# Hybrid attention and DeltaNet step on one core: values of head pair 1 ahead of the keys of pair 2, and no clearing of the diagonal blocks

## The chip, the core and the metric

The kernel runs on one core of a Trainium2 chip. It is one launch; its time is the device time of that launch in microseconds, as the median of some runs. TensorE (PE), VectorE (DVE), ScalarE (ACT), GpSimd (POOL) and SyncE (SP, which here only issues DMAs) each work off their own queue in order and wait for one another by semaphores.

## What is computed

A two-layer decoder trunk for a prompt of 1024 tokens and a sample group of 8 sequences with 4 tokens each, all of width 1024. Layer 0 is sliding-window attention, layer 1 gated DeltaNet with 8 query/key heads and 16 value heads of 128; each branch has a SiLU gate. The change touches layer 1 for the prompt, cut here to what matters:

```python
xqkv, z, a, b = split(h @ w_in)
q, k, v = split(silu(short_causal_conv(xqkv)))
q, k = l2_norm(q), l2_norm(k)                      # 8 heads, each used by two value heads
lower = where(strict, (k_i . k_j) beta_i exp(gc_i - gc_j), 0)
w = triangular_solve(lower + I, [v beta, k beta exp(gc)])
u = w_v - w_k @ S                                  # chunk by chunk
o = (q exp(gc)) @ S + (q k^T decay) @ u
S = S exp(g_total) + k_decayed^T @ u
y = (rms_norm(o) * silu(z)) @ w_out
```

The reference uses chunks of 64 tokens; the kernel does the same sum with 8 chunks of 128 (`NB`).

## The kernel before

The kernel computes in fp32. Its large products split both operands into a high and a low part of type fp32r and add three matmuls (`h2hi` with `wh`, `h2lo` with `wh`, `h2hi` with `wl`). The input of layer 1 lies in SBUF, transposed, in three token groups of 384, 384 and 288 columns (`GRP`). A projection of 128 output columns is therefore 8 x 3 matmuls for each group, 72 in all. Its weights come as two loads of 256 KB (`wr`); ACT rounds them to `wh`, POOL makes `wl`.

Layer 1 goes by head pairs: pair r is one query/key head and two value heads. For each pair the kernel needs these stages:

- `proj_kq` projects a key (k) or a query (q), `proj_v` the two values (here v1a and v1b for pair 1), `proj_z` one gate (z2 and z3 for pair 1). `conv` (L1655) takes a projection from PSUM on ACT (`XR`), applies the four taps (`taps`, one on ACT and three on DVE, into `kT`, `qT` or `vT`) and a SiLU; for the samples (`samples`) it takes a small path over PE, POOL and some small DMAs. The `vT` tiles are transposed into `vo` (`turn`).
- `decay_blocks` makes the decay matrices `DP`. `solve` (L1832) computes the norms of the keys and the 8 triangular systems `UZ` (two heads by 128 x 128, four tiles of four systems) as `UZ<-ps_lg,sj,DP`. It writes the 32 x 32 blocks on the diagonals of all systems to DRAM (`Ld`).
- `invert` (L1882) loads them as `X` (64 small systems side by side), sets their diagonals to one on POOL, and inverts them by 31 pairs of DVE instructions (`tmp<-X`, `X<-X,tmp`), which follow one another through a single buffer. The result goes through DRAM (`Xdd`) into `Xc`. Before the change POOL also clears the diagonal blocks of `UZ` here (L1892 to L1896): 16 memsets for each pair.
- `diagonal` (L1914) and `blocks` (L1936), together the block solve: POOL spreads `Xc` into `Xd`, a tile that is zero outside its diagonal blocks; PE multiplies `UZ` by it (`ps_lg<-Xd,UZ`); ACT negates the product into `M`; DVE transposes `Xd` over the whole of `UZ`. Then six rounds of small products (`ps_lg<-UZ,M`), which DVE copies back into `UZ`, fill the blocks off the diagonal.
- `decayed` makes the query-key matrices in `DP`.
- `chain` (L1984) goes through the 8 chunks of a pair in order: PE multiplies key by state (`ps_mi<-S,kT`), DVE corrects the values (`vo<-ps_mi,nEg,vo`), PE applies the solved system (`ps_ob<-vo,UZ`), DVE scales the result (`us<-ps_ob,sd`), PE multiplies it by the keys (`ps_mi<-us,ktok`), DVE makes the next state (`S`). `output` adds `ps_mi<-S,qT` and `ps_mi<-uo,DP`; `gating` normalises the output on ACT, DVE and POOL (`rst`, `fo`), transposes it (`ps_tr<-cst,vo`) and gates it.

The order of all this is made while the program is built. `Core` (L96) keeps a clock for each engine with rough costs, and every helper is a generator that says when it could go on. Projections are the main line: after each matmul the waiting generators may put their instructions into the queues. Two words matter. `weave` adds a generator to those that wait. `until(condition)` holds the main line: as long as the condition is false, only generators add instructions, so nothing of the main line stands among them in PE's queue.

The main line of layer 1 is the loop over r at L2157. Round r starts with the chain of pair r - 1 and the query of pair r, then two gates, then the key of pair r + 1 and the two values of pair r, in the order that `VK` picks:

```python
for what in "vk" if r in VK else "kv":
    if what == "k":
        until(lambda: finished[0] >= r - 1)
        proj_kq(r + 1, states[r + 1], (0,))
    else:
        until(lambda: gs is not None and gated[0] >= 4 * (r - 1))
        proj_v(r, states[r])
```

So the key of pair r + 1 is held until the chain of pair r - 1 is finished (its tiles are used again), and the values of pair r until pair r - 2 is gated. `plan` (L1633) puts the weight loads into the same order. The chain of a pair needs its values and the first tile of its solved systems; the block solve of a pair needs its keys.

Of the kernel before, what the change touches and what calls it, by code (L numbers as in the profile page):

```python
# [219 lines left out]
def body(tc, I, O, cst_ap, dbg=None):  # L220
    nc = tc.nc
# [22 lines left out]
    SW = (1, 16)  # L244
    MS = (32, 15)
    AH, AI = (a / 10 for a in AM)
    VK = ()
    MM = (0, 20)
    ORDER = [("q", 2), ("q", 3), ("q", 4), ("q", 5), ("z", 0), ("k", 1), ("z", 1), ("z", 2), ("q", 6), ("q", 7),
             ("z", 3), ("z", 4), ("z", 5), ("z", 6), ("z", 7)]  # L250
# [234 lines left out]
    def weave(gen, name, hq=None):  # L485

        rank = KR[hq][name] if hq is not None else K[name]
        i = 0
        while i < len(jobs) and jobs[i][3] <= rank:
            i += 1  # L490
        jobs.insert(i, [lambda: True, gen, name, rank])
# [25 lines left out]
    def plain():  # L517
        return not isinstance(nc, Core)

    def ready(*ts):  # L520
        return lambda: plain() or nc.ready(ts) <= nc.free["tensor"]

    def soon(*ts):
        return lambda: plain() or nc.ready(ts) <= nc.free["tensor"] + AH

    def idle(eng, *ts):
        return lambda: plain() or max(nc.free[eng], nc.ready(ts)) <= nc.free["tensor"] + AI
# [7 lines left out]
    def bank(tag):  # L535

        q = held.setdefault(tag, [])
        yield lambda: len(q) < banks[tag] or q[-banks[tag]] is None
        t = psb(tag)
        q.append(t.tensor.name)  # L540
        yield lambda: plain() or nc.after(nc.used, t, "tensor") <= nc.free["tensor"]
        return t

    def give(tag, t):
        q = held[tag]
        q[q.index(t.tensor.name)] = None
# [215 lines left out]
    if True:  # L762
# [524 lines left out]
        nc = Core(tc)  # L1287
# [346 lines left out]
    for r in range(HQ):  # L1634
        pz, pv = [4096 + 2 * r * P, 4096 + (2 * r + 1) * P], [2 * HQ * P + 2 * r * P, 2 * HQ * P + (2 * r + 1) * P]
        pk = [(HQ + r + 1) * P]
        plan += [r * P] + (pz + (pv + pk if r in VK else pk + pv) if r + 1 < HQ else pv + pz)
    hhi, hlo = h2hi, h2lo
# [4 lines left out]
    if True:  # L1643
# [163 lines left out]
        def spare(hq):  # L1807

            return "mi" if hq == 0 else "lg"
# [22 lines left out]
        def solve(hq, st):  # L1832
# [25 lines left out]
            for c4 in range(2):  # L1858
# [19 lines left out]
                give(lg, pk)  # L1878
            st["built"] = True
            weave(invert(hq, st, Ld, Xdd), "invert", hq)  # L1880

        def invert(hq, st, Ld, Xdd):  # L1882
            UZ, lg = st["UZ"], spare(hq)
            yield lambda: inverted[0] == hq


            X = gs.tile([64, 32, 32], F32, tag="X", name="X")
            tmp = gs.tile([64, 256], F32, tag="tmp", name="tmp")
            nc.sync.dma_start(X, Ld)
            yield soon(X)  # L1890
            nc.gpsimd.memset(X.rearrange("p i c -> p (i c)")[:, 0:1024:33], 1.0)
            for cp_ in range(4):  # L1892
                uv = UZ[cp_].rearrange("p h c i -> p (h c) i")
                for b in range(4):
                    bs = slice(32 * b, 32 * b + 32)
                    nc.gpsimd.memset(uv[bs, :, bs], 0.0)  # L1896
            yield soon(X)
            for k in range(31):
                n, m = 31 - k, k + 1
                tv = tmp[:, 0:n * m].rearrange("p (i c) -> p i c", c=m)  # L1900
                yield idle("vector")
                nc.vector.tensor_tensor(tv, X[:, k, k + 1:].unsqueeze(2).to_broadcast([64, n, m]),
                                        X[:, k, 0:m].unsqueeze(1).to_broadcast([64, n, m]), ALU.mult)
                nc.vector.tensor_tensor(X[:, k + 1:, 0:m], X[:, k + 1:, 0:m], tv, ALU.subtract)
            nc.sync.dma_start(Xdd, X)
            inverted[0] += 1
            yield lambda: solved[0] == hq
            Xc = gs.tile([P, 16, 32], F32, tag="Xc", name="Xc")
            for b in range(4):
                nc.sync.dma_start(Xc[32 * b:32 * b + 32], Xdd[16 * b:16 * b + 16].rearrange("q i c -> i q c"))  # L1910

            lg, Ms, uzs = "lg", [], [t_.rearrange("p h c i -> p (h c) i") for t_ in UZ]

            def diagonal():  # L1914

                for cp_, uz in enumerate(uzs):
                    xd = Xd[cp_ % 2]
                    yield soon(Xc)
                    for b in range(4):
                        bs = slice(32 * b, 32 * b + 32)  # L1920
                        nc.gpsimd.tensor_tensor(xd[bs, :, bs], Xc[bs, 4 * cp_:4 * cp_ + 4, :],
                                                C["lo32"][bs, :].unsqueeze(1).to_broadcast([32, 4, 32]), ALU.mult)
                    yield lambda: st.get("pairs", 0) >= cp_ - 2
                    yield ready(xd)
                    pm = yield from bank(lg)
                    pmv = pm.rearrange("p (q i) -> p q i", q=4)
                    for q in range(4):
                        nc.tensor.matmul(pmv[:, q, 0:96], uz[:, q, :], xd[:, q, 0:96], start=True, stop=True)
                    yield soon(pm)
                    M = gs.tile([P, 4, 96], F32, tag="M", name="M", bufs=3)  # L1930
                    nc.scalar.activation(M, pmv[:, :, 0:96], AF.Copy, scale=-1.0)
                    give(lg, pm)
                    nc.vector.transpose(uz.rearrange("p q i -> p (q i)"), xd.rearrange("p q i -> p (q i)"))
                    Ms.append(M)

            def blocks():  # L1936


                for v in range(6):
                    parts = [(v - s, 64 - 32 * s) for s in range(3) if 0 <= v - s < 4]  # L1940
                    yield lambda: len(Ms) > parts[0][0]
                    yield ready(*[Ms[cp_] for cp_, _ in parts], *[UZ[cp_] for cp_, _ in parts])
                    pz = yield from bank(lg)
                    pzv = pz.rearrange("p (q i) -> p q i", q=4)
                    for q in range(4):
                        for cp_, r0 in reversed(parts):
                            rs, cs = slice(r0, r0 + 32), slice(r0 + 32, P)
                            nc.tensor.matmul(pzv[rs, q, cs], Ms[cp_][:, q, rs], uzs[cp_][:, q, cs], start=True, stop=True,
                                             skip_group_check=True)
                    yield soon(pz)  # L1950
                    for cp_, r0 in reversed(parts):
                        rs, cs = slice(r0, r0 + 32), slice(r0 + 32, P)
                        nc.vector.tensor_copy(uzs[cp_][rs, :, cs], pzv[rs, :, cs])
                    give(lg, pz)
                    st["pairs"] = max(0, v - 1)
                solved[0] += 1

            weave(blocks(), "blocks", hq)
            weave(diagonal(), "blocks", hq)

        def decayed(hq, st):
# [195 lines left out]
        for r in range(HQ):  # L2157
# [5 lines left out]
            if r + 1 < HQ:  # L2163
# [4 lines left out]
                weave(solve(r + 1, states[r + 1]), "solve", r + 1)  # L2168
                for what in "vk" if r in VK else "kv":
                    if what == "k":  # L2170
# [509 lines left out]
    nc = nc.nc  # L2680
# [36 lines left out]
```

## Time and profile before

| | |
|---|---|
| runs before | 1739.1, 1732.38, 1730.36 us; median 1732.38 |
| the profiled execution, its own time | 1730.22 us |
| its span | 1728.1 us |
| mean granted PE clock | 0.983 |

A profile's times count from the start of its span. In rows of instructions the columns are start, length, engine, line, operation, output and inputs by the program's names, shapes and count, then the idle time of the engine before them and what ended it. Nearly all instructions have line 89, the wrapper that records them, so rows are told apart by their tiles. An fp32 product appears as two records; a row with x4 can be two of them. Rows of groups give the count, busy time in us and the mean of one in ns.

### The profile page before, as it was taken

Reading aid. Unit: us, or ns where it says so; the run is one execution under the profiler, and the core shown is the slowest. Engines: PE = TensorE matmul, PEld = TensorE weight load, DVE = VectorE, ACT = ScalarE, POOL = GpSimd, SP = SyncE. Lnnn points to the kernel's source line nnn. Section 1 sums busy time; section 2 is a strip of 40 time slices with the busy share of each in tenths; the row PEclk is TensorE's granted clock in tenths of the full one; section 3 lists DMA queues with packets and bytes.
Section 4 is the critical chain, followed back from the end, with each engine's and each line's share of the span. In section 5 each row is a group of like instructions: output and inputs, shape, how many; then the busy total and the mean of one; then the engine's idle time right before and its main releaser. Section 6 shows DMA issues by size and latency. Waiting matters only on the chain. (4 is left out here: it accounts for less than half of the span.)

```text
span 1728.1 us, 31800 instructions
## 1 busy us (share of the span) xinstructions
PE 1628.6 (94%) x10666; PEld 1432.1 (83%) x10666; DVE 1207.9 (70%) x3538; ACT 862.0 (50%) x2514; POOL 603.2 (35%) x1170
## 2 busy tenths in 40 slices
PE   6999999998999899799999999999999998989897
PEld 5988888986777889689989999899998996667685
DVE  4526675564565678877887789778798876357677
ACT  4625555444334565256554665654756555332332
POOL 2601111112122334354443544545345454332322
PEclk9999999999999999899999999999999999999999
DMA  9542121233233232132412323224232137764785
GB/s 330 152 134 72 52 58 50 55 98 106 85 130 103 81 79 67 53 88 56 126 36 75 102 59 107 69 77 112 50 107 62 46 97 211 228 200 130 233 277 184
DMA packets 281573, 191.77 MB, mean 111 GB/s; under 512 B 98362, under 2 KB 253882, under 8 KB 281379
## 3 DMA queue, kind: packets, MB, share of 16 engines
q1 hardware_dynamic: 281410, 189.75, 38.1%
q8 instruction: 84, 1.38, 0.3%
q14 instruction: 79, 0.64, 0.1%
HBM read 144.68 MB, written 47.04 MB: 111 GB/s over the span
## 5 line engine op out<-in xcount | busy, mean ns | idle before, releaser
L89 PE MATMUL ps_pj<-h2hi,wl 128*128 128x384 f32 (+1 forms) x1128 | 380.4, 337 | 2.2 <-POOL wl L89 2.2
L89 PE MATMUL ps_pj<-h2hi,wh 128*128 128x384 f32 (+1 forms) x1128 | 378.3, 335 | 2.1 <-ACT wh L89 2.1
L89 PE MATMUL ps_pj<-h2lo,wh 128*128 128x384 f32 (+1 forms) x1128 | 379.4, 336 | 0.0
L89 POOL TENSOR_TENSOR wl<-wr,wh 128x512 fp32r<-128x512 f32 x122 | 164.4, 1348 | 517.5 <-ACT wh L89 432.9
L89 PEld LDWEIGHTS ps_pj<-h2hi,wl 128*128 128x128 f32 x1128 | 213.6, 189 | 6.2 <-POOL wl L89 3.1
L89 PEld LDWEIGHTS ps_pj<-h2hi,wh 128*128 128x128 f32 x1128 | 213.5, 189 | 4.3 <-ACT wh L89 2.4
L89 PEld LDWEIGHTS ps_pj<-h2lo,wh 128*128 128x128 f32 x1128 | 213.5, 189 | 3.2
L89 POOL TENSOR_TENSOR xt<-xt,y 128x512 f32<-128x512 f32 (+1 forms) x48 | 63.9, 1333 | 188.2 <-DVE y L89 165.1
L89 PE MATMUL ps_pj<-hlo,wh 128*128 128x384 f32 (+1 forms) x360 | 119.0, 331 | 0.0
L89 PE MATMUL ps_pj<-hhi,wh 128*128 128x384 f32 (+1 forms) x360 | 118.4, 329 | 0.0
L89 PE MATMUL ps_pj<-hhi,wl 128*128 128x384 f32 (+1 forms) x360 | 117.9, 328 | 0.0
L89 DVE SCALAR_TENSOR_TENSOR vT<-XR,cT,vT 128x384 f32<-128x384 f32 (+1 forms) x144 | 93.0, 658 | 29.0 <-ACT vT L89 27.1
L89 DVE TENSOR_TENSOR tmp<-X 64x31 f32<-64x31 f32 (+15 forms) x248 | 94.0, 379 | 10.4 <-POOL X L89 7.1
L89 DVE TENSOR_TENSOR X<-X,tmp 64x31 f32<-64x31 f32 (+15 forms) x248 | 94.6, 381 | 8.5
L89 ACT CAST wh<-wr 128x512 fp32r<-128x512 f32 x122 | 75.1, 616 | 16.4 <-PE ps_pj L89 12.0
L89 PEld LDWEIGHTS ps_pj<-hlo,wh 128*128 128x128 f32 x360 | 67.7, 188 | 11.2 <-issue 11.1
L89 ACT COPY XR<-ps_pj 128x384 f32<-128x384 f32 (+1 forms) x96 | 43.0, 448 | 55.9 <-PE ps_pj L89 55.7
L89 POOL TENSOR_TENSOR Xd<-Xc,cst 32x128 f32<-32x128 f32 x128 | 63.4, 495 | 21.2 <-DMA Xc<-Xdd 10.4
L89 PEld LDWEIGHTS ps_pj<-hhi,wh 128*128 128x128 f32 x360 | 67.7, 188 | 2.7 <-issue 2.7
L89 ACT ACTIVATE prob<-prob,nm 128x256 f32<-128x256 f32 (+1 forms) x128 | 62.2, 489 | 14.8 <-DVE nm L89 14.6
L89 PEld LDWEIGHTS ps_pj<-hhi,wl 128*128 128x128 f32 x360 | 67.7, 188 | 2.1 <-issue 2.1
L89 ACT ACTIVATE vo<-vo,fo 128x128 f32<-128x128 f32 x128 | 42.3, 392 | 54.0 <-POOL fo L89 54.0
(574 smaller groups left out, 4218.1 us busy)
## 6 DMA issues: line engine op xcount, KB each, us to landing
wr<-in_gdn_w_in SPq DMA_DIRECT2D x96, 256.0 KB
S<-in_state_gdn_s SPq DMA_DIRECT2D x40, 256.0 KB
xt<-in_x_prompt SPq DMA_DIRECT2D x16, 512.0 KB
wm<-in_w_mod SPq DMA_DIRECT2D x16, 512.0 KB
wr<-in_swa_w_in SPq DMA_DIRECT2D x64, 128.0 KB
wmod<-in_w_mod SPq DMA_DIRECT2D x32, 256.0 KB
wm<-in_w_mod SPq DMA_DIRECT2D x32, 256.0 KB
DP<-gcr SPq DMA_DIRECT2D x64, 128.0 KB
```

The source lines that it names most:

```text
L89: inst = fn(*args, **kwargs)
```

## The change

`VK` names the rounds in which the values go first. It was empty and now holds 1: in round 1 the order q1, z2, z3, k2, v1a, v1b becomes q1, z2, z3, v1a, v1b, k2, for the weight loads too. And `invert` no longer clears the diagonal blocks of `UZ`, for any pair. Where the zeros were read, their product gets other numbers in the rows of its own block; these are later multiplied by blocks of `UZ` that are still zero, so the result is the same. The blank line that the diff adds in `diagonal` has no meaning.

```diff
@@ -244,7 +244,7 @@
     SW = (1, 16)
     MS = (32, 15)
     AH, AI = (a / 10 for a in AM)
-    VK = ()
+    VK = (1,)
     MM = (0, 20)
@@ -1889,11 +1889,6 @@
             nc.sync.dma_start(X, Ld)
             yield soon(X)
             nc.gpsimd.memset(X.rearrange("p i c -> p (i c)")[:, 0:1024:33], 1.0)
-            for cp_ in range(4):
-                uv = UZ[cp_].rearrange("p h c i -> p (h c) i")
-                for b in range(4):
-                    bs = slice(32 * b, 32 * b + 32)
-                    nc.gpsimd.memset(uv[bs, :, bs], 0.0)
             yield soon(X)
             for k in range(31):
                 n, m = 31 - k, k + 1
```

As the order follows from the clocks of `Core`, every queue differs behind these places: the built orders of the two kernels agree up to the first 3165 of PE's 7724 entries.

## The prediction

> **What bounds the kernel now.** I read the page first, then the windows by round, then the timelines of TensorE (PE), VectorE (DVE) and GpSimd (POOL) where a round is longer than the others.
>
> ```profile
> span 1728.1 us, 31800 instructions
> PE 1628.6 (94%) x10666; PEld 1432.1 (83%) x10666; DVE 1207.9 (70%) x3538; ACT 862.0 (50%) x2514; POOL 603.2 (35%) x1170
> ```
>
> PE is busy in 94% of the span, far ahead of the rest, so what counts is where PE's queue stands still. Matmul spans overlap, so idle time alone understates it; rounds show it better. A round is what the kernel issues from one query projection to the next: six projections of 72 matmuls and the other pairs' work between them. Its borders (658.0, 797.4, 908.6, ...) are where the matmuls that write `ps_pj` go from 288 columns back to 384 for a query group. The columns of the windows view are window, length, busy time of PE, weight loads, DVE, ACT, POOL, then clock, DMA share, GB/s.
>
> ```profile
> 658.00:797.40 139.40, 125.42 (x896) 112.80 (x896) 114.74 (x313) 67.06 (x207) 57.43 (x142) 0.96 0.26 69
> 797.40:908.60 111.20, 107.45 (x755) 101.65 (x754) 90.33 (x251) 62.13 (x195) 50.12 (x126) 0.98 0.30 78
> 908.60:1019.10 110.50, 107.86 (x759) 102.83 (x758) 87.50 (x247) 62.40 (x197) 49.45 (x126) 0.98 0.32 83
> 1019.10:1128.70 109.60, 107.35 (x761) 100.73 (x760) 92.62 (x251) 65.07 (x203) 51.95 (x126) 1.00 0.30 80
> 1128.70:1235.70 107.00, 105.62 (x751) 99.41 (x750) 84.45 (x234) 62.30 (x198) 50.55 (x126) 1.00 0.30 83
> 1235.70:1346.80 111.10, 107.57 (x764) 101.31 (x763) 94.64 (x261) 61.26 (x194) 50.41 (x126) 1.00 0.31 81
> ...
> 705.20:754.10 48.90, 38.21 (x280) 29.30 (x281) 40.00 (x122) 17.09 (x62) 14.74 (x52) 0.90 0.19 51
> 754.10:797.40 43.30, 42.95 (x311) 41.01 (x310) 33.89 (x82) 30.21 (x87) 16.53 (x34) 1.00 0.25 67
> ```
>
> Round 1, the one that the change reorders, takes 139.4 us; the next five take 109.9 on average ((111.2 + 110.5 + 109.6 + 107.0 + 111.1) / 5). The surplus of 29.5 us sits in 705.2 to 754.1: clock 0.90, and no projection matmul in 48.9 us. There the kernel waits, while it is built, until the chain of pair 0 is finished before it may write the keys of pair 2 into PE's queue, so PE has only that chain, step by step behind DVE, and the rest of two block solves.
>
> ```profile
> 720.48 0.75 PE L89 MATMUL ps_ob<-vo,UZ 128*128 128x128 f32 x4 [0.58 <-DVE vo L89]
> ...
> 726.91 0.75 PE L89 MATMUL ps_ob<-vo,UZ 128*128 128x128 f32 x4 [0.44 <-DVE vo L89]
> ...
> 733.13 0.75 PE L89 MATMUL ps_ob<-vo,UZ 128*128 128x128 f32 x4 [0.44 <-DVE vo L89]
> ...
> 737.40 0.74 PE L89 MATMUL ps_ob<-vo,UZ 128*128 128x128 f32 x4 [0.44 <-DVE vo L89]
> 738.85 0.70 PE L89 MATMUL ps_mi<-us,ktok 128*128 128x256 f32 x2 [0.70 <-DVE us L89]
> ...
> 740.51 0.60 PE L89 MATMUL ps_mi<-S,qT 128*128 128x256 f32 x2
> 740.95 0.61 PE L89 MATMUL ps_mi<-uo,DP 128*128 128x128 f32 x4
> 741.39 1.03 PE L89 MATMUL ps_lg<-Xd,UZ 128*128 128x96 f32 x8
> 742.26 0.62 PE L89 MATMUL ps_mi<-S,kT 128*128 128x256 f32 x2
> ...
> 743.68 0.44 PE L89 MATMUL ps_lg<-UZ,M 128*32 128x32 f32 x8
> ...
> 745.15 0.61 PE L89 MATMUL ps_lg<-UZ,M 128*32 128x64 f32 x16 [0.39 <-DVE UZ L89]
> ...
> 748.53 0.85 PE L89 MATMUL ps_lg<-UZ,M 128*32 128x96 f32 x24
> ...
> 754.11 0.42 PE L89 MATMUL ps_pj<-h2hi,wh 128*128 128x384 f32 x1
> ```
>
> One step of the chain runs from one `ps_ob<-vo,UZ` to the next: 733.13 to 737.40 is 4.3 us when DVE is free, 720.48 to 726.91 is 6.4 us while DVE also works at the inversion of pair 1. At 754.11 the keys of pair 2 begin.
>
> **The change part by part.** Part one: the two value projections of pair 1 go ahead of the keys of pair 2. They need no finished chain, so in the built order the chain of pair 0 now lies between the matmuls of z3, v1a and v1b.
>
> ```profile
> 697.39 0.29 PE L89 MATMUL ps_pj<-h2hi,wh 128*128 128x288 f32 x1
> 697.52 0.30 PE L89 MATMUL ps_pj<-h2lo,wh 128*128 128x288 f32 x1
> ...
> 754.72 0.34 PE L89 MATMUL ps_pj<-h2hi,wh 128*128 128x384 f32 x1
> 754.89 0.34 PE L89 MATMUL ps_pj<-h2lo,wh 128*128 128x384 f32 x1
> ```
>
> A projection is 48 matmuls of 384 columns, 0.17 to 0.18 us apart, and 24 of 288, 0.13 apart: 48 x 0.175 + 24 x 0.13 = 11.5 us. The two bring 23 us of cover. What can be won is what round 1 loses: the 29.5 us less the work that it has beyond a usual round. That is one more block solve, since pairs 0 and 1 are both solved there: four groups of `Xd,UZ` at 0.87 (741.39 to 742.26) and six of `UZ,M`, two each of 0.44, 0.61 and 0.85 (743.68, 745.15, 748.53), 3.5 + 3.8 = 7.3. So 22.2 us can go, and 23 us of cover is just enough: term -22.2.
>
> First cost: the end of the chain still stands bare. In the built order the last two steps of pair 0 come after the last matmul of v1b with nothing between them: 24 operations, each two records in the trace. On an unloaded DVE they take a step (4.3) and the piece from 737.40 to the end of `uo,DP` at 740.95 + 0.61, 4.2: 8.5 us. Their own work is 5 products 256 wide at 0.44 (740.51 to 740.95) and 19 operations 128 wide at 0.22 (two in 740.95 to 741.39), 6.4. Lost: 2.1; with step and tail both slowed as 6.4 to 4.3, 12.7, it is 6.3. I take 3.5, as the inversion of pair 1 ends about there. Queued behind it on PE are the keys of pair 2, and behind those the system of pair 2.
>
> Second cost: what is late next. The keys of pair 2 come two projections later, but chain 1 does not move with them. In the built order the block solve of pair 2 slips from k3 and v2a into q3 and z6, and the chain of pair 2 starts in z6 instead of q3. The keys of pair 4 wait for that chain, so behind z7 stands a second bare stretch: 34 operations, two and a half steps. By the same rows it lasts 2 x 4.3 + 2.7 = 11.3 (2.7 from `us,ktok` at 738.85 to 741.56) to 2 x 6.4 + 2.7 = 15.5, and holds 8 x 0.44 + 26 x 0.22 = 9.2 of work. Lost: 2.1 to 6.3; I take 4.5, because half of the inversion of pair 3 stands among those steps.
>
> Third cost: DVE. Its taps of the two value convolutions now lie among the steps of chain 0.
>
> ```profile
> L89 DVE SCALAR_TENSOR_TENSOR vT<-XR,cT,vT 128x384 f32<-128x384 f32 (+1 forms) x144 | 93.0, 658 | 29.0 <-ACT vT L89 27.1
> ...
> L89 DVE COPY UZ<-ps_lg 32x128 f32<-32x128 f32 (+2 forms) x96 | 40.0, 417 | 9.9 <-PE ps_lg L89 7.9
> ...
> L89 DVE STREAM_TRANSPOSE UZ<-Xd 128x512 f32<-128x512 f32 x32 | 22.7, 709 | 18.4 <-PE ps_lg L89 15.7 <-POOL fo L89 1.2 <-POOL Xd L89 1.1
> ```
>
> Two projections have 18 of the 144 taps: 18 x 0.658 = 11.8 us. The copies and transposes of one block solve move out to q2: 12 x 0.417 + 4 x 0.709 = 7.8. Between the first and the last scaling of chain 0
>
> ```profile
> 709.34 0.61 DVE L89 TENSOR_SCALAR us<-ps_ob,sd 128x128 f32<-128x128 f32 x2
> ...
> 750.78 0.61 DVE L89 TENSOR_SCALAR us<-ps_ob,sd 128x128 f32<-128x128 f32 x2
> ```
>
> lie 41.4 us; DVE needs 4.0 more, about 45. PE's queue holds, by the built order, 96 projection matmuls of 384 columns and 55 of 288 between the same points (24.0), 20 wide products (8.8), 56 operations 128 wide (12.3) and the end of a block solve (0.9): 46. Two engines equally full, with a chain that goes to and fro between them, lose something: 0, or half of the added taps, 6. I take 3.
>
> Part two: GpSimd's clears.
>
> ```profile
> 691.93 3.71 POOL L89 MEMSET UZ<- 32x128 f32 x16
> 695.71 4.35 POOL L89 TENSOR_TENSOR Xd<-Xc,cst 32x128 f32<-32x128 f32 x8
> ```
>
> Sixteen clears hold POOL from 691.93 to 695.71, 3.8 us for each pair, and the next `Xd` of the block solve of pair 0 stands right behind them. Without them that solve can come up to 3.8 us sooner. Elsewhere PE waits little for POOL:
>
> ```profile
> PE ps_lg L89 <- POOL Xd L89: 4.2, 3, 1.9
> ...
> PE ps_pj L89 <- POOL wl L89: 2.2, 2, 1.5
> ```
>
> The cover is now z3's and v1a's matmuls, so I take 0, bounds 0 and -3.8; without cover the whole 3.8 counts once. Nothing else needs the zeros: the product that read them is later multiplied by rows that are zero. DVE doesn't gain either: the same multiplication of the inversion takes 0.29 at 694.73, with the clears beside it, and 0.29 at 728.04, with none.
>
> ```profile
> 694.73 0.29 DVE L89 TENSOR_TENSOR tmp<-X 64x135 f32<-64x135 f32 x1
> ...
> 728.04 0.29 DVE L89 TENSOR_TENSOR tmp<-X 64x135 f32<-64x135 f32 x1
> ```
>
> The moved projections take their transfers along: each has two weight loads of 256 KB, one load of old convolution state and five small stores on SP, and its two `wl` splits and eight sample operations on POOL. Weights are planned in the same changed order, and from 705.2 to 754.1 the DMA engines are 0.19 and POOL 14.74 of 48.9 us busy, so they cost nothing; if that cover failed, one late split costs what the longest wait for `wl` is, 1.5 us.
>
> Sum: -22.2 + 3.5 + 4.5 + 3 + 0 = -11.2. The profiled execution took 1730.2 us, its span of 1728.1 and 2.1 around it, so 1719.0. The three runs lie at 1730.4, 1732.4 and 1739.1, the profile at their lower end, where a run of the changed kernel can come out as well: 1719.
>
> [...] In 705.2 to 754.1 the clock is 0.90 and four records of `uo,DP` take 0.61 at 740.95. [...]
>
> **The rivals.** Full cover, 1708: both bare ends cost their lower bound, the block solve comes forward and DVE hides its taps: -22.2 + 2.1 + 2.1 - 3.8 = -21.8. For it: PE's rounds 2 to 6 run close to their work. Against: the two bare ends stand in the built order.
>
> The wait only moves, 1728: DVE, not missing PE work, holds chain 0. Then the 11.8 us of taps lengthen that chain in full, the bare ends cost what I take for them, and -22.2 + 11.8 + 3.5 + 4.5 = -2.4. For it: DVE is busy 40.0 of the 48.9 us. Against: the step from 733.13 takes 4.3 where the one from 720.48 takes 6.4, so the chain alone leaves DVE room.
>
> Slower, 1742: pair 2 becomes the late one. Its inversion stands behind chain 1 on DVE.
>
> ```profile
> L89 DVE TENSOR_TENSOR tmp<-X 64x31 f32<-64x31 f32 (+15 forms) x248 | 94.0, 379 | 10.4 <-POOL X L89 7.1
> L89 DVE TENSOR_TENSOR X<-X,tmp 64x31 f32<-64x31 f32 (+15 forms) x248 | 94.6, 381 | 8.5
> ```
>
> Per pair that is (94.0 + 94.6) / 8 = 23.6 us of DVE, followed by a block solve and eight steps of 6.4, all before the keys of pair 4. If the chain of pair 2 ends some 30 us after z7's last matmul, the old loss of 22.2 is back in round 3, with the first bare end (6.3) and the dense DVE (6) on top: -22.2 + 22.2 + 12.3 = +12.3, and from there on it decides. Against: only two and a half steps stand bare behind z7, not eight.
>
> **How the numbers follow.** Forecast 0.50, full cover 0.12, wait moves 0.22, slower 0.16. The likeliest case's own range follows from its bounds: -22.2 + 2.1 + 2.1 + 0 - 3.8 to -22.2 + 6.3 + 6.3 + 6 is 1708 to 1727. 0.5%, what a measurement of this kernel can tell from no change, is 8.7 us: below 1723.7 is faster, above 1741 slower. Faster: most of the forecast (0.44), full cover (0.12) and a little of the third, 0.58. Slower: 0.15. Within: 0.27. The 8-in-10 range goes from just under full cover to near the slower case, 1707 to 1740.
>
> **What would show it.** Right: round 1 near 118 us instead of 139.4, with z3, v1a and v1b matmuls between the steps of chain 0 and a clock near 1.00; a bare stretch under 10 us before the keys of pair 2 and one of 11 to 15 us before the keys of pair 4; rounds 4 to 6 as before; no POOL clears of `UZ`. Wrong: a bare stretch of 25 us or more in round 3 (slower), steps of 8 us in round 1 with PE waiting for `us` and `vo` (wait moves), or a gain spread over all rounds, which would mean that the clears were on the path.

## The result and the profile after

The changed kernel takes 1722.28 us in the median of 5 runs (1719.15 to 1723.84), the kernel before 1736.34 of 5 (1730.36 to 1739.1). The ratio is 0.9921 with a 95% interval of 0.9897 to 0.9946: 13.7 us, with 9.4 to 17.9 as bounds. A second comparison, `changed_again` below, gives 0.9931 (0.9912 to 0.9949). The profiled execution took 1723.84 us.

The head of the changed kernel's page, span and busy times:

```profile
span 1721.9 us, 31655 instructions
PE 1630.3 (95%) x10666; PEld 1435.0 (83%) x10666; DVE 1210.1 (70%) x3538; ACT 862.9 (50%) x2514; POOL 587.1 (34%) x1042
```

PE, DVE and ACT have as many instructions as before. POOL has 128 fewer, the clears, which kept it busy for 25.2 us before; its busy time falls by only 16 us, as its other instructions together took 9 us longer. The windows of the changed kernel by round, cut as before at the first matmul of each query (columns as in the prediction), and below them its two bare stretches:

```profile
664.40:783.70 119.30, 112.62 (x831) 104.95 (x830) 102.14 (x269) 58.93 (x184) 55.84 (x126) 1.00 0.30 79
783.70:889.60 105.90, 102.16 (x682) 97.78 (x681) 86.96 (x248) 67.88 (x215) 45.90 (x98) 0.98 0.31 84
889.60:1015.80 126.20, 120.27 (x899) 110.14 (x899) 105.77 (x287) 63.83 (x198) 53.31 (x122) 0.99 0.27 72
1015.80:1124.00 108.20, 107.78 (x761) 101.04 (x760) 91.78 (x252) 64.95 (x202) 48.26 (x110) 1.00 0.31 82
1124.00:1230.80 106.80, 106.15 (x758) 100.71 (x758) 88.62 (x246) 63.19 (x199) 48.83 (x110) 1.00 0.32 82
1230.80:1337.60 106.80, 106.06 (x756) 100.42 (x755) 87.73 (x251) 61.69 (x194) 47.31 (x110) 1.00 0.30 83
1337.60:1412.50 74.90, 73.28 (x470) 68.80 (x469) 66.82 (x181) 48.69 (x164) 36.77 (x90) 1.00 0.24 67
753.30:763.50 10.20, 6.63 (x40) 4.78 (x38) 6.02 (x22) 6.86 (x28) 5.38 (x20) 1.00 0.64 161
949.60:963.50 13.90, 11.04 (x59) 8.74 (x58) 9.27 (x33) 6.72 (x30) 4.63 (x17) 0.88 0.43 102
```

Round 1 falls from 139.4 to 119.3 us with a clock of 1.00 in place of 0.96, round 2 from 111.2 to 105.9, and round 3 grows from 110.5 to 126.2. The chain of pair 0 now runs between projection matmuls, as PE's timeline of the changed kernel shows:

```profile
726.03 0.60 PE L89 MATMUL ps_ob<-vo,UZ 128*128 128x128 f32 x4
726.39 0.42 PE L89 MATMUL ps_pj<-h2hi,wh 128*128 128x384 f32 x1
...
732.52 0.61 PE L89 MATMUL ps_ob<-vo,UZ 128*128 128x128 f32 x4
...
753.24 0.29 PE L89 MATMUL ps_pj<-h2hi,wl 128*128 128x288 f32 x1
...
753.77 0.61 PE L89 MATMUL ps_ob<-vo,UZ 128*128 128x128 f32 x4
755.91 0.70 PE L89 MATMUL ps_mi<-us,ktok 128*128 128x256 f32 x2 [1.52 <-DVE us L89]
...
759.03 0.75 PE L89 MATMUL ps_ob<-vo,UZ 128*128 128x128 f32 x4 [0.45 <-DVE vo L89]
...
763.06 0.60 PE L89 MATMUL ps_tr<-cst,vo 128*128 128x128 f32 x4
763.42 0.42 PE L89 MATMUL ps_pj<-h2hi,wh 128*128 128x384 f32 x1
```

A step of the chain takes 6.5 us there (726.03 to 732.52), and PE works on projections meanwhile. The last matmul of v1b starts at 753.24, the keys of pair 2 at 763.42: between them stand the last two steps, bare, for 10.2 us.

**One number for the lost time.** A round also changes when work moves in or out of it. So the experiments use a second measure as well: for every matmul of a round, the time until the next one starts, less the median of that time over all matmuls of its kind (same product, same width) in that trace, where that is positive; the sum is the *loss* of the round. Before, round 1 lost 33.1 us and rounds 2 to 6 lost 13.7 on average (15.2, 14.6, 13.2, 11.4, 14.2). After, round 1 lost 19.1, rounds 2 and 3 together 36.2 (29.8 before), rounds 4 to 7 together 42.2 (47.2 before): 110.1 in rounds 1 to 7 became 97.5. The loss of a shorter stretch is summed in the same way.

Rounds and losses of all kernels, one profile each, in us. The ratios are of all runs, each profile is of one: that of `clears_charged_not_run` is the longest of its 12 runs, that of `values_first_1_3_and_5` the shortest of its 12. "Last" is the time from the first matmul of z15 to the end of the span:

| kernel | ratio to before (95%) | r1 | r2 | r3 | r4 to r7 | r1 to r7 | last | loss r1 | loss r2 + r3 | loss r4 to r7 |
|---|---|---|---|---|---|---|---|---|---|---|
| before | 1 | 139.4 | 111.2 | 110.5 | 402.1 | 763.2 | 306.9 | 33.1 | 29.8 | 47.2 |
| changed | 0.9921 (0.9897, 0.9946) | 119.3 | 105.9 | 126.2 | 396.7 | 748.1 | 309.4 | 19.1 | 36.2 | 42.2 |
| changed_again | 0.9931 (0.9912, 0.9949) | 119.5 | 106.0 | 125.7 | 396.1 | 747.3 | 307.7 | 19.3 | 35.7 | 41.6 |
| order_only | 1.0049 (1.003, 1.0068) | 121.1 | 118.7 | 113.8 | 409.2 | 762.8 | 315.8 | 20.9 | 37.3 | 54.8 |
| no_clears_only | 1.0107 (1.0082, 1.0131) | 141.1 | 114.2 | 109.3 | 415.5 | 780.1 | 307.2 | 35.3 | 31.8 | 59.0 |
| clears_charged_not_run | 0.9979 (0.9965, 0.9993) | 138.6 | 111.0 | 110.9 | 400.1 | 760.6 | 309.3 | 32.1 | 29.9 | 45.1 |
| changed_with_clears_uncharged | 0.998 (0.996, 1.0001) | 123.7 | 108.9 | 125.5 | 401.3 | 759.4 | 305.5 | 23.2 | 38.2 | 46.5 |
| order_only_clears_charged_not_run | 0.9993 (0.9975, 1.0011) | 122.3 | 119.6 | 112.2 | 399.5 | 753.6 | 314.7 | 22.3 | 36.6 | 44.9 |
| values_first_1_and_3 | 0.9985 (0.9971, 0.9999) | 119.4 | 103.8 | 117.3 | 409.2 | 749.7 | 315.5 | 19.1 | 29.5 | 52.6 |
| values_first_1_3_and_5 | 1.0001 (0.9985, 1.0018) | 121.2 | 104.0 | 117.6 | 419.2 | 762.0 | 302.2 | 20.8 | 29.7 | 60.7 |
| changed_without_taps_of_pair_1 | 0.9914 (0.9889, 0.9939) | 118.5 | 106.6 | 125.2 | 397.0 | 747.3 | 308.7 | 18.3 | 35.9 | 42.5 |
| one_value_first | 1.0168 (1.0151, 1.0186) | 130.2 | 113.3 | 125.5 | 413.3 | 782.3 | 308.1 | 26.9 | 41.9 | 56.9 |
| outputs_of_pair_1_later | 0.9941 (0.9922, 0.9961) | 119.1 | 113.9 | 116.3 | 398.2 | 747.5 | 307.3 | 18.9 | 34.9 | 42.7 |
| chain_of_pair_1_later | 1.0083 (1.0063, 1.0104) | 119.2 | 110.7 | 118.7 | 420.7 | 769.3 | 312.2 | 19.0 | 33.8 | 63.9 |

### The profile page after: what moved, and what is told of

The parts are those of the page before. It is cut to its first block, busy times and chain, and to the rows that moved or that the text cites. A ratio compares the mean times of both kernels' runs of the same rounds, so it can differ in the third digit from the quotient of the medians.

```text
span 1721.9 us, 31655 instructions
## 1 busy us (share of the span) xinstructions
PE 1630.3 (95%) x10666; PEld 1435.0 (83%) x10666; DVE 1210.1 (70%) x3538; ACT 862.9 (50%) x2514; POOL 587.1 (34%) x1042
## 5 line engine op out<-in xcount | busy, mean ns | idle before, releaser
L89 PE MATMUL ps_pj<-hlo,wh 128*128 128x384 f32 (+1 forms) x360 | 119.3, 331 | 0.0
L89 DVE SCALAR_TENSOR_TENSOR vT<-XR,cT,vT 128x384 f32<-128x384 f32 (+1 forms) x144 | 96.8, 680 | 25.1 <-ACT vT L89 23.8
L89 DVE TENSOR_TENSOR tmp<-X 64x31 f32<-64x31 f32 (+15 forms) x248 | 97.7, 394 | 7.2 <-POOL X L89 3.9
L89 PEld LDWEIGHTS ps_pj<-hlo,wh 128*128 128x128 f32 x360 | 67.9, 189 | 11.2 <-issue 11.1
L89 ACT ACTIVATE prob<-prob,nm 128x256 f32<-128x256 f32 (+1 forms) x128 | 62.2, 489 | 14.8 <-DVE nm L89 14.6
L89 ACT ACTIVATE qe<-ps_mi,Eg 128x128 f32<-128x128 f32 x112 | 35.0, 364 | 66.4 <-PE ps_mi L89 66.4
```

The lines of the kernel that those rows point to most:

```text
L89: inst = fn(*args, **kwargs)
```

## The experiments

Each of the two parts also changes what the kernel's own clocks charge, and so the order of everything behind it. The first runs separate three things: the order, the clears on the chip, and the charge for the clears.

**The first part alone.** `VK` is changed, the clears stay.

```diff
-    VK = ()
+    VK = (1,)
```

> Only the first half of the change: the values of pair 1 go ahead of the keys of pair 2, GpSimd keeps its clears. In the built order 24 operations stand bare behind v1b as in the changed kernel, but no stretch of 34 behind z7. Theory (the gain is the filled wait of round 1, the clears are worth nothing): -22.2 + 3.5 + 3 = about -15.7 us against the kernel before, ratio 0.991, round 1 near 119 us and round 3 near 118 instead of the 126.2 of the changed kernel. Rival one (the clears are the gain): ratio 1.000, with round 1 shortened and the time lost again in rounds 2 and 3. Rival two (the stretch behind z7 costs nothing): ratio as the changed kernel, 0.992, and round 3 no shorter than its 126.

Measured: 1743.59 us against 1735.03, ratio 1.0049. Round 1 came near to what was expected, 121.1 us. Round 3, without the stretch behind z7, took 113.8 where 118 was expected, but round 2 took 118.7, rounds 4 to 7 took 7.1 us more than before, and the last stage 8.9 more. The theory holds for round 1; the sum made of it falls. By its number the first rival is the nearest. A run below, with this order and without the clears, shows that about 9.7 us of this kernel's time are the clears; what else it lost behind round 1 came with the new order.

**The second part alone.** The five lines of the clears go, `VK` stays empty.

> Only the second half of the change: the clears go, the keys stay ahead of the values. The charge of the clears on the kernel's own clocks goes too, so the order is made anew: behind z3 now stand 79 operations without a projection matmul instead of 146. Theory (what counts is how long the chain of pair 0 stands without projections): the loss of 22.2 us shrinks with the number of operations, 22.2 x 79 / 146 = 12.0, so about -10 us, ratio 0.994, all of it in round 1. Rival one (the clears themselves hold the solves): 3.8 us in each of eight pairs, up to -30 us, ratio down to 0.983, spread over the rounds. Rival two (the length of that stretch doesn't matter): 1.000.

Measured: 1752.34 us against 1735.03, ratio 1.0107. No expectation had a slower kernel; for round 1 the second rival, that the length of the stretch doesn't matter, comes out. The window of round 1 of this kernel:

```profile
662.50:803.60 141.10, 126.63 (x897) 113.34 (x897) 113.68 (x302) 66.96 (x205) 54.55 (x126) 0.95 0.27 67
```

With 79 operations bare behind z3 instead of 146 it is no shorter than before (139.4). The bare stretch itself, from the last matmul of z3 to the keys of pair 2, lasts 44.9 us (710.77 to 755.63) instead of 51.1 (702.99 to 754.11), and loses 25.6 instead of 23.9. The operations that moved out of the stretch had not made it long; they had filled it. It lasts until the chain has finished, and half the operations did not make it lose less. Another 10 us went in round 7 (84.4 against 74.4), in a new order of its own.

**The clears alone, with the order held.** The clears are charged and not issued. In the built order TensorE, VectorE, ScalarE and SyncE have the same entries in the same sequence as before.

```diff
-                    nc.gpsimd.memset(uv[bs, :, bs], 0.0)
+                    nc.issued("gpsimd", "memset", None, (uv[bs, :, bs],), {})
```

> The kernel before, but the 128 clears aren't issued, while their cost stays on the kernel's own clocks: TensorE, VectorE, ScalarE and SyncE keep the order of the kernel before, entry by entry. This is the worth of the clears on the chip alone. Theory: 0, at most -3.8 us (round 1, ahead of the block solve of pair 0): ratio 0.998 to 1.000. Rival (the clears hold every block solve): 8 x 3.8 = -30 us, ratio 0.983, or some part of that spread over the rounds.

Measured: 0.9979, 3.6 us (1.2 to 6.1). By its number the theory's lower end holds, but not by its place: round 1, where all of it was to be, gained 0.8 us. The product behind the clears of round 1 has no wait in the kernel before:

```profile
698.59 1.03 PE L89 MATMUL ps_lg<-Xd,UZ 128*128 128x96 f32 x8
```

The rest of the 3.6 us stands in no single place of the trace.

**The order of the changed kernel, with the clears.** The clears are issued and not charged, so that TensorE, VectorE and ScalarE keep the order of the changed kernel.

```diff
+            for cp_ in range(4):
+                uv = UZ[cp_].rearrange("p h c i -> p (h c) i")
+                for b in range(4):
+                    bs = slice(32 * b, 32 * b + 32)
+                    nc.quiet(nc.nc.gpsimd.memset(uv[bs, :, bs], 0.0).ins)
```

(`quiet` only keeps them in program order on GpSimd.)

> The changed kernel with the 128 clears issued again on GpSimd, but not charged on the kernel's own clocks: TensorE, VectorE and ScalarE keep the order of the changed kernel, entry by entry. It separates what the clears cost on the chip from what their charge does to the order. Theory (as with the kernel before, where the clears were worth 0.21%, 3.6 us): 0 to 6 us above the changed kernel, ratio to the kernel before 0.992 to 0.996. Rival (the clears are most of the gain of the changed kernel): back at 1.000 or above.

Measured: 0.998, between the theory and its rival. So the clears are worth 0.5 to 0.6% here, 8.5 or 10.2 us (0.998 less 0.9931 or 0.9921, of 1733), more than the 3.6 in the old order and above what the theory allowed. The intervals of the two figures meet; that the clears cost more in this order rests on the next run and on the traces as well. Rounds 1 to 7 took 759.4 instead of 748.1, and the trace shows where. POOL's timeline of this kernel, around the block solve of pair 0, then the gating in round 2:

```profile
698.01 0.16 POOL L89 MEMSET X<- 64x32 f32 x1 [1.00 <-DMA smd<-th]
698.07 3.73 POOL L1902 MEMSET UZ<- 32x128 f32 x16
701.86 4.07 POOL L89 TENSOR_TENSOR Xd<-Xc,cst 32x128 f32<-32x128 f32 x8
...
843.73 0.16 POOL L89 MEMSET X<- 64x32 f32 x1 [1.78 <-DMA X<-Ld]
843.79 3.80 POOL L1902 MEMSET UZ<- 32x128 f32 x16
847.67 0.20 POOL L89 TENSOR_TENSOR rst<-rsw 128x4 f32<-128x4 f32 x1
...
851.47 0.20 POOL L89 TENSOR_TENSOR fo<-rst,rsw 128x4 f32<-128x4 f32 x1
```

PE's timeline of the same kernel at both places:

```profile
703.38 2.03 PE L89 MATMUL ps_lg<-Xd,UZ 128*128 128x96 f32 x8 [2.41 <-POOL Xd L89]
...
852.16 1.35 PE L89 MATMUL ps_tr<-cst,vo 128*128 128x128 f32 x4 [3.53 <-ACT vo L89]
```

And the changed kernel's POOL and PE at the same two places:

```profile
697.39 0.15 POOL L89 MEMSET X<- 64x32 f32 x1 [0.99 <-DMA X<-Ld]
697.62 2.04 POOL L89 TENSOR_TENSOR Xd<-Xc,cst 32x128 f32<-32x128 f32 x4
...
837.75 0.17 POOL L89 MEMSET X<- 64x32 f32 x1 [0.90 <-DMA X<-Ld]
837.91 0.20 POOL L89 TENSOR_TENSOR rst<-rsw 128x4 f32<-128x4 f32 x1
...
841.18 0.27 POOL L89 TENSOR_TENSOR fo<-rst,rsw 128x4 f32<-128x4 f32 x1
```

```profile
700.77 1.03 PE L89 MATMUL ps_lg<-Xd,UZ 128*128 128x96 f32 x8
...
843.25 0.60 PE L89 MATMUL ps_tr<-cst,vo 128*128 128x128 f32 x4
```

With the clears the next `Xd` starts at 701.86, behind 3.73 us of memsets, and PE stands 2.41 us with the product at the head of its queue. All the matmuls of z3 that come behind it in the queue wait as well (the next one starts at 705.12): they are not cover. Without the clears the product has no wait. The place costs more than the 2.41 us of the wait: from 702.60 to 709.50 the granted clock is 0.51. The windows of the kernel with the clears:

```profile
699.20:702.60 3.40, 1.77 (x15) 1.17 (x14) 2.33 (x8) 0.15 (x1) 2.87 (x14) 1.00 0.33 108
702.60:709.50 6.90, 6.12 (x34) 5.51 (x35) 2.50 (x6) 0.49 (x1) 4.72 (x11) 0.51 0.00 0
```

In the changed kernel the clock is 1.00 there, and the same matmuls take 4.8 us less. In round 2 the sixteen clears of pair 2 stand between the diagonal of `X` and the `rst` of a gating; the gating's `fo` is late, ACT scales late, and PE waits 3.53 us for `vo`. Without them the transposition runs between the matmuls of z5 with no wait.

PE's order is the same in the two kernels but for 10 of 10666 records, so each matmul can be set against its twin. The kernel with the clears falls back by 4.8 us at the block solve and by 5.7 at the gating, of which 3.0 come back later in round 2 (the changed kernel has the clock at 0.51 from 872.7 to 876.2, the other has 1.00 at these matmuls). It falls back by 2.1 more in round 5 and by 2.9 in round 7. There the clears stand ahead of the small convolution of the samples on POOL; ACT waits for its result (`us`) with the copy of `uo` behind it in its queue, and PE waits for `uo`:

```profile
1137.60 3.83 POOL L1902 MEMSET UZ<- 32x128 f32 x16
1141.49 0.43 POOL L89 COPY XS<-XR 128x32 f32<-128x32 f32 x1
...
1144.75 0.23 ACT L89 ACTIVATE us<-us 128x32 f32<-128x32 f32 x1 [6.76 <-POOL us L89]
...
1146.71 0.71 PE L89 MATMUL ps_mi<-uo,DP 128*128 128x128 f32 x4 [1.87 <-ACT uo L89]
```

**The first order without the clears.** As `clears_charged_not_run`, with `VK = (1,)`.

> The values of pair 1 first, in the very order that the kernel with the charged clears had (ratio 1.0049), but without the clears. Theory (that kernel is slow because of its order in the later stages, not because of the clears): 1.001 to 1.005. Rival (the values-first order makes the clears harmful, so that both parts need one another on the chip): 0.992, as the changed kernel.

Measured: 0.9993 against 1.0049 for the same order with clears: 0.56%, 9.7 us. It lies between the theory and the rival. Again the clears cost about 10 us in a values-first order, though at other places: here round 1 gains nothing without them, and the loss of rounds 4 to 7 falls from 54.8 to 44.9. What the theory says of the order holds in part: without its clears this kernel is still some 11 us slower than the changed one, of which 5.3 us are in the last stage (314.7 against 309.4) and 5.5 in rounds 1 to 7.

**The taps.** For pair 1's values the three VectorE taps are charged and not issued.

```diff
-                        nc.vector.scalar_tensor_tensor(up, XR[:, a0 + i:e + i], cw[:, i, ct:ct + 1], up, ALU.mult, ALU.add)
+                        args_ = (up, XR[:, a0 + i:e + i], cw[:, i, ct:ct + 1], up, ALU.mult, ALU.add)
+                        if ct in (18, 19):
+                            nc.issued("vector", "scalar_tensor_tensor", None, args_, {})
+                        else:
+                            nc.vector.scalar_tensor_tensor(*args_)
```

> The changed kernel without the last three of the four taps of the convolution of pair 1's values (18 VectorE instructions, 11.8 us), which stay charged on the kernel's own clocks, so that all orders stay. It measures the third cost of the prediction, the taps among the steps of chain 0. Prediction: 3 us, bounds 0 and 6: ratio to the kernel before 0.989 to 0.992, round 1 at 113 to 119 instead of 119.3. Rival (VectorE holds chain 0, the wait only moves): 11.8 us, ratio 0.985 to 0.986, round 1 near 108.

Measured: 0.9914, which the intervals can't tell from the changed kernel. The window of round 1 of this kernel:

```profile
664.50:783.00 118.50, 112.53 (x829) 104.87 (x829) 93.72 (x251) 58.75 (x184) 52.83 (x126) 1.00 0.30 79
```

DVE has 18 instructions and 8.4 us less (102.14 to 93.72), and the round is 0.8 us shorter. The chain does wait for VectorE at single steps, but the added taps don't lengthen it; the rival is refuted.

**Values first in more rounds.** `VK = (1, 3)` and `VK = (1, 3, 5)`, no clears.

> The changed kernel, with the values first in round 3 too (pair 3 ahead of the keys of pair 4). In the built order the stretch of 34 operations behind z7 is gone, the 24 behind v1b stay, and no stretch of over 18 stands in the rounds after. Theory (the stretch behind z7 is the second cost, 4.5 us predicted, up to 7.8 by the trace of the changed kernel): 4.5 to 8 us below the changed kernel, ratio to the kernel before 0.988 to 0.990, round 3 near 119 us instead of 126.2. Rival one (that stretch is hidden anyway): 0.992, as the changed kernel. Rival two (the wait only moves on by two rounds each time): a stretch in round 5 costs the same again, 0.992, and round 5 is longer than 107.

> No clears, values first in rounds 1, 3 and 5. Up to the middle of round 5 its built order is that of the kernel with rounds 1 and 3, and the last stage has the order of the changed kernel. Theory (the last stage costs 298 us in the order of the changed kernel and 304 in that of rounds 1 and 3, whatever stands before): rounds 1 to 4 as with rounds 1 and 3 (119, 104, 117, 115), last stage 298, together 0.994 to 0.996. Rival one (the last stage is slower by what happened earlier, not by its own order): 304 again, 0.998. Rival two (each further swap pays as the first): below 0.992.

Measured: 0.9985 and 1.0001. Without the stretch behind z7 the loss of rounds 2 and 3 is 29.5, as before the change (29.8; 36.2 in the changed kernel). But rounds 4 to 7 lose 52.6 instead of 42.2, and the last stage takes 315.5. With round 5 swapped too, the last stage is short again, 302.2, and shorter than the theory had it (the theory's 298 and 304 count from another place; by the table they are 309.4 and 315.5). But rounds 4 to 7 lose 60.7. The nearest of the theories is the second rival of the first run: the loss moves on to later rounds, though as many small waits. Apart from the one behind v1b, no stretch of over 6 us without projections is left in rounds 1 to 7 of either kernel.

**Half of the cover.** In round 1 the order is q1, z2, z3, v1a, k2, v1b.

```diff
-    (pv + pk if r in VK else pk + pv)
+    (pv[:1] + pk + pv[1:] if r in VK else pk + pv)
...
-                for what in "vk" if r in VK else "kv":
+                for what in "vkw" if r in VK else "kv":
```

(`w` projects the second value.)

> No clears, and in round 1 only the first value projection of pair 1 goes ahead of the keys of pair 2, the second one behind them (half of the cover). In the built order 55 operations stand bare behind v1a, and 106 behind z7 instead of 34. Theory (a stretch costs in proportion to the steps of the chain that stand bare in it, wherever it is): round 1 near 127 us, 8 above the changed kernel; the stretch behind z7 near that of the kernel before behind z3, so some 15 us more than in the changed kernel in round 3; together 1.003 to 1.008. It is the slower rival of the prediction, made on purpose. Rival (half the cover is half the gain, and the stretch behind z7 is hidden): 0.996.

Measured: 1.0168, by the medians 28 us slower than before and slower than the theory said. The windows of this kernel: round 1, then its bare stretches behind v1a and behind z7.

```profile
664.50:794.70 130.20, 121.51 (x881) 109.78 (x881) 106.82 (x277) 65.04 (x198) 55.90 (x126) 0.97 0.28 72
733.50:761.30 27.80, 20.67 (x94) 14.91 (x93) 20.87 (x68) 15.10 (x56) 12.92 (x40) 0.88 0.35 92
958.50:988.80 30.30, 24.26 (x204) 18.23 (x202) 24.00 (x77) 12.96 (x48) 8.85 (x40) 1.00 0.21 61
```

Half the cover is half the gain of round 1: 139.4, 130.2, 119.3. Behind z7 stands a stretch of 30.3 us: the slower rival of the prediction exists, at the place that it named. Rounds 2 and 3 lose 41.9 us where the kernel before loses 29.8, and rounds 4 to 7 lose 9.7 more than before (round 7 takes 84.1, as in `no_clears_only`). The two profiles are 26.8 us apart; 6.5 of that lie ahead of round 1, where nothing was changed (last section).

**Two other orders of the changed kernel, and itself again.** One rank of the planner is altered in each of the first two.

```diff
-    KR = [..., {'chain': 0, 'output': 3, ...
+    KR = [..., {'chain': 0, 'output': 10, ...
```

```diff
-    KR = [..., {'chain': 0, 'output': 3, ...
+    KR = [..., {'chain': 30, 'output': 3, ...
```

> The changed kernel with one rank of the planner altered: the outputs of pair 1 (8 groups of two products and their additions) give way to other waiting work (rank 10 instead of 3). In the built order the stretch behind z7 has 22 operations instead of 34, and from round 6 on the order is that of the changed kernel. Theory (the stretch costs 4.7 us for 34 operations): 13.9 x 22 / 34 = 9.0 us long, 1.7 to 5 us gained, round 3 at 121 to 125, ratio 0.989 to 0.991. Rival (what is taken from that stretch is lost again in rounds 3 to 5): 0.992 or above.

> The changed kernel with another rank altered: the chain of pair 1 gives way to other waiting work (rank 30 instead of 0). In the built order no stretch of over 16 operations is left behind z7; everything from round 2 on is ordered anew. Theory (the second cost is the stretch behind z7): 4.7 us gained in round 3, ratio 0.988 to 0.990. Rival (each new order of rounds 4 to 7 and of the last stage brings its own waits, as with the values first in rounds 1 and 3): 0.997 to 1.000, with round 3 short and the loss behind it.

> The changed kernel itself once more, beside the other three and the kernel before on one chip, to tie the scales together and to see how far two profiles of one order differ. Expected: ratio 0.990 to 0.994, rounds 1 to 3 within 2 us of 119.3, 105.9 and 126.2.

Measured: 0.9941, 1.0083 and 0.9931. With 22 operations behind z7 round 3 falls from 125.7 to 116.3, far more than expected, and round 2 rises from 106.0 to 113.9: rounds 2 and 3 together lose 34.9 instead of 35.7. The rival is nearer, and gave too late a place: the loss came back in the round before. With no stretch behind z7, rounds 2 and 3 lose 33.8, but rounds 4 to 7 lose 63.9, 22 us more: that is the rival's mechanism, and 1.0083 is slower than even the rival said. The two profiles of the changed kernel agree within 0.5 us in every one of rounds 1 to 7, so differences of several us in a round are not scatter. No version measured is faster than the changed kernel beyond the intervals.

## Why the prediction was right, point by point

The forecast said 1719 and the runs say 1722, -11.2 us and -13.7; direction and size were right. Its parts were not all, and that the sum agrees is in part luck: some terms were too large, others too small, and the clears and the order were worth other amounts than it gave them.

- **The bound.** Right. Round 1 came out at 119.3 us ("near 118"), by chain 0 between projections, in every kernel that puts both values first (118.5 to 123.7).
- **The term -22.2** was somewhat too large. It took the surplus of 29.5 less one block solve of 7.3. By the loss, round 1 had 33.1 - 13.7 = 19.4 us to give; the other 10 of the surplus were work that stayed or moved to another round. In the changed kernel round 1 lost 19.1, that is 14.0 less; it kept 5.0 for the bare end (below) and 0.8 for the taps, so 14.0 + 5.0 + 0.8 = 19.8 were filled, which is the 19.4 within the accuracy of this.
- **First cost.** Right in its length, somewhat too small in its loss. The bare end lasts 10.2 us (predicted 8.5 to 12.7; the sign "under 10" is missed by 0.2). The prediction reckoned its work at 6.4 us, with two records for each of the 24 operations. But 11 of these are transposes, which have one record each (the four of a gating are the x4 at 763.06), so it has 37 records and 5.1 us of work by the medians of their kinds. It lost 5.0; taken was 3.5, within bounds of 2.1 and 6.3.
- **Second cost.** Right at its place, somewhat too small, and not to be had back. The last z7 matmul and the keys of pair 4 in the changed kernel's PE timeline:

```profile
949.57 0.29 PE L89 MATMUL ps_pj<-h2hi,wl 128*128 128x288 f32 x1
949.70 0.59 PE L89 MATMUL ps_mi<-us,ktok 128*128 128x256 f32 x2
...
952.99 0.75 PE L89 MATMUL ps_ob<-vo,UZ 128*128 128x128 f32 x4 [0.86 <-DVE vo L89]
954.96 1.22 PE L89 MATMUL ps_mi<-us,ktok 128*128 128x256 f32 x2 [1.23 <-DVE us L89]
955.98 1.06 PE L89 MATMUL ps_mi<-S,qT 128*128 128x256 f32 x2
...
963.47 0.42 PE L89 MATMUL ps_pj<-h2hi,wh 128*128 128x384 f32 x1
```

  The stretch lasts 13.9 us (predicted 11.3 to 15.5). With 12 transposes among its 34 operations it has 7.9 us of work and not 9.2, and lost 6.0; taken was 4.5, bounds 2.1 and 6.3. Rounds 2 and 3 together lost 6.4 more than before. What the prediction did not see is that the loss doesn't go with the stretch. Two orders without it (`order_only`, `chain_of_pair_1_later`) and one with a shorter one (`outputs_of_pair_1_later`) still lose 33.8 to 37.3 in rounds 2 and 3; `values_first_1_and_3` is back at 29.5 there and loses 10.4 more in rounds 4 to 7. Each of these orders differs in other places as well, so why the loss comes back is not shown.
- **Third cost.** Too large: 0.8 us measured, 3 taken, inside its bounds of 0 and 6. Nearly all of the taps fitted beside PE's work.
- **The clears at 0.** This is the step that failed, in its reason. "The cover is now z3's and v1a's matmuls, so I take 0": the matmuls of z3 stood behind the waiting product in PE's queue, through its 2.41 us, and did not cover it. In the old order the product that the prediction looked at came late enough for its tile to be ready (698.59, no wait), and all the clears together were worth 3.6 us. In the new order they would have cost 8.5 to 10: in the block solve, with the clock at 0.51 behind the wait, and, not thought of at all, in what else stands behind them on POOL, a gating in round 2 and the samples' convolution in rounds 5 and 7. The bound of -3.8 counted one place of one pair.
- **The sum.** By the route on which the clears go first and the order second, the runs give -3.6 and then 13.7 - 3.6 = -10.1 (-8.3 by the second comparison), and the prediction had 0 and -11.2. By the other route the order brings -3.5, which its interval (0.996 to 1.0001) can't tell from nothing, and the clears the rest. The parts don't simply add. The prediction's number for the order is right only because the clears were removed with it; that is the luck in it.
- **Rounds 4 to 6 as before.** Nearly right for this kernel: 396.7 us for rounds 4 to 7 against 402.1; with the clears issued they take 401.3, so the gain there is theirs. But it was an assumption that nothing in the prediction bore. The first part alone loses 54.8 there instead of 42.2 (44.9 without its clears), and three other orders with both values first lose 52.6 to 63.9. The reorder shortens round 1 by 16 to 21 us in every kernel that has it; how much of it is left at the end was decided by orders that neither the diff nor the argument speaks of.
- **The rivals.** "The wait only moves" is refuted by the run without taps. "Full cover" is refuted by the two bare stretches. "Slower" did not happen here; `one_value_first` shows that it was one order away.
- **The clock.** The sum has no term for it. In the second end it was 0.53 for 3.4 us, by estimate 1.6 of the 6.0 us lost there (last section); in the first end it stayed at 1.00.

## What to carry to other kernels

Matmuls behind a waiting one in PE's queue were no cover (2.41 us at the block solve of pair 0); an off-path engine's small instructions cost little while what they held up was not yet due (the clears, 3.6 us in the old order) and more when it was (8.5 to 10 us in the new one), so price them again in a new order. The stretch in which PE had only the chain and the block solves lasted until the chain was through: moving independent work into it took round 1 from 139.4 to 119.3 us, while taking other work out of it gained nothing (44.9 us long instead of 51.1, with 25.6 lost instead of 23.9). Where a planner orders the queues by its own costs, removing an instruction changes every later order: to learn what the instruction is worth, keep its charge and drop it, or drop the charge and keep it.

## What the hardware showed that was not expected

**A clock of 0.53 in the second bare end.** Two windows of the changed kernel, just before and just after 954.90, in the stretch behind z7:

```profile
951.50:954.90 3.40, 1.37 (x6) 0.78 (x6) 3.19 (x15) 0.39 (x2) 0.34 (x2) 0.97 0.83 212
954.90:958.30 3.40, 3.34 (x10) 2.85 (x11) 1.49 (x5) 0.68 (x3) 2.38 (x11) 0.53 0.33 79
```

For 3.4 us the granted clock is 0.53, and the products 256 wide at 954.96 and 955.98 take 1.22 and 1.06 us, where the one at 949.70 takes 0.59; behind it, from 958.30 to 963.50, the clock is 1.00 again. In the 3.4 us before, PE was busy for 1.37, and its longest idle time was 1.23 us. In the kernel with the clears PE was busy for 1.77 of the 3.40 us ahead of its 6.9 us at 0.51 (699.20 to 702.60 above). In the first bare end it was busy for 6.63 of 10.20 us, and the clock stayed at 1.00. What brings the clock down, no run here shows. At 0.53 the 3.4 us cost some 1.6 by estimate (3.4 x 0.47), about a quarter of what the second bare end lost.

**The stretch ahead of the change spreads the runs.** The windows from the first query and key to the first matmul of q1, in the kernel before and in `changed_again`:

```profile
536.00:657.80 121.80, 108.96 (x689) 103.07 (x688) 82.47 (x231) 69.68 (x183) 40.23 (x72) 0.99 0.29 79
```

```profile
536.80:665.60 128.80, 113.81 (x689) 108.19 (x688) 83.80 (x237) 70.37 (x184) 38.53 (x56) 0.93 0.28 74
```

PE's order is the same there, and the granted clock is 0.99 in one and 0.93 in the other, with 7.0 us between them. In the other twelve profiles, all with this order, the stretch takes 122.6 to 129.5 us; 127.4 in `clears_charged_not_run`, which keeps PE's order of before. The profile of before happened to be a quick one at this place, which is why the two profiles differ by only 6.4 us (1730.22 and 1723.84) where the medians differ by 13.7; the sum of rounds 1 to 7 differs by 15.1.
